# RWKV chunk chain with keys and queries side by side in the left operand, group norm by token, inversion transposes from fp16 parts

## The chip, the cores and the metric

One core of one Trainium2 chip runs the whole kernel. Five engines work side by side, each with its own list of instructions in a fixed order: TensorE (PE in the profile; its weight loads are PEld), VectorE (DVE), ScalarE (ACT), GpSimd (POOL) and SyncE (SP, which issues most of the DMAs here). They wait for each other by semaphores. The metric is the device time of one execution in microseconds; lower is better.

## What is computed

The reference is one decoder block on 512 tokens of width 2048. Two branches read the same normalised input: an RWKV-7 time mixing with 16 heads of 64 channels, and a sliding-window attention. Their gated sum is added to the input, and a gated convolutional feed-forward network follows. The change lies in the RWKV branch. Cut to that:

```python
def step(state, inp):
    r_t, k_t, v_t, w_t, ka_t, kb_t = inp          # ka = -kk, kb = kk * a
    sa = jnp.einsum('bhvk,bhk->bhv', state, ka_t)
    state = (state * w_t[:, :, None, :] + sa[..., None] * kb_t[:, :, None, :]
             + v_t[..., None] * k_t[:, :, None, :])
    y = jnp.einsum('bhvk,bhk->bhv', state, r_t)
    return state, y
...
mu = jnp.mean(y, axis=-1, keepdims=True)
var = jnp.mean(jnp.square(y - mu), axis=-1, keepdims=True)
y = ((y - mu) * lax.rsqrt(var + GN_EPS)).reshape(B, S, RW_DIM)
y = y * gn_w + gn_b
bonus = jnp.sum(rh * kh * r_k, axis=-1, keepdims=True) * vh
out = (y + bonus.reshape(B, S, RW_DIM)) * g
```

The recurrence runs over tokens; `y` is then normalised over the 64 channels of each head and token (the group norm).

## The kernel before, in words

The kernel takes two heads at a time: eight pairs, each on 128 partitions (64 per head). The 512 tokens are cut into eight chunks of 64. `early(p)` makes a pair's inputs: it projects key, receptance and value (`ztile`, three projections of 48 matmul rows each: L256 to L258), normalises the key by head, makes decays, and multiplies the bonus. The key norm is computed by matmuls with two selecting columns (`head_stats`, L330), an inverse square root on VectorE (`rsqrt_small`), a transpose (L333), and a round trip through DRAM that spreads the 8 x 128 values over partitions (`head_rows`, L337 and L341).

`late(p)` is the recurrence. It has these steps:

- `BKK` holds the two key-like vectors of both heads by channel, scaled by inverse decay; `BAR` holds the two query-like ones (`kk` and `r`), scaled by decay, with zeros where the other head's channels are. One matmul per chunk (L643) gives all products of keys and queries. Masks make `AB` (strictly lower, L646) and `MM` (with the diagonal, L647) from it.
- A triangular 64 x 64 matrix per head and chunk is inverted by doubling: levels of block size 2 to 32 (L687/L688 in fp16 with a high and a low part, `mm3`). The result is written to `BX` in fp32. After each level but the last, the whole of `BX` is transposed in fp32 (L734), and `split` makes the fp16 high part on ScalarE (L210) and the low part on VectorE (L211), which reads the high part.
- The chain over chunks. For each chunk and head: G = `AB`ᵀ`SV` (L741), where `SV` holds the state in 64 partitions and the values in the other 64; U = `BX`ᵀG (L745); the state's increment = `KK`ᵀ`UV` (L752), where `UV` holds U in 64 partitions and the values in the other 64; then the next state (L754) on VectorE. G, the increment and later y of the two heads go to the two halves of the PSUM partitions, so each of these matmuls has a 128 x 64 left operand.
- The output y = `UV`ᵀ`MM` + `SV`ᵀ`BAR` (L762, L764), also per head and chunk, comes out with channels on partitions.

`final(p)` does the group norm: a centring matmul with a 128 x 128 matrix on the high and low parts of y (L772, L773), squares, `head_stats` and `head_rows` with their DRAM round trip, then scale, shift, bonus and the output gate (`lora`), and a DMA to DRAM issued by POOL (L788).

The loop runs late(p), early(p+1), final(p) and then three gate projections. A scheduler then orders each engine's list: projections of early(p+1) and the gates stand between the small matmuls of late(p). PSUM buffers are three `bulk` tiles, three `acc` tiles and two `chn` tiles. POOL also issues the DMAs that add up pairs of weights for later stages (L232), each behind a load that SP issues (L231).

## Time and profile before

| | |
|---|---|
| median of three runs | 2905.28 us (2903.66 to 2905.93) |
| the profiled execution | 2901.93 us, its span 2900.2 us |
| granted TensorE clock, mean | 0.998 |
| RWKV stage with its pairs | about 300 to 1175 us of the span |
| L734, the inversion's fp32 transposes | 256 rows, 275 ns mean |
| L741, L752, L762, L764 together | 960 rows of 128 x 64 left operands |

How to read it: a row of the profile names the source line, the engine, the operation, the tile it writes and those it reads. An fp32 matmul stands as two rows, a transpose and an fp16 or fp32r matmul as one. Matmuls are pipelined: the duration of a row is longer than the distance to the start of the next. In the timeline, the number in front is the start in microseconds, the next is the time from there to the end of the group, and xN is how many like rows are merged. In a line of the view by windows stand the length of the window, and then for each engine the busy time and the number of instructions in it.

### The profile page before, as it was taken

Reading aid. Unit: us, or ns where it says so; the run is one execution under the profiler, and the core shown is the slowest. Engines: PE = TensorE matmul, PEld = TensorE weight load, DVE = VectorE, ACT = ScalarE, POOL = GpSimd, SP = SyncE. Lnnn points to the kernel's source line nnn. Section 1 sums busy time; section 2 is a strip of 40 time slices with the busy share of each in tenths; the row PEclk is TensorE's granted clock in tenths of the full one; section 3 lists DMA queues with packets and bytes.
Section 4 is the critical chain, followed back from the end, with each engine's and each line's share of the span. In section 5 each row is a group of like instructions: output and inputs, shape, how many; then the busy total and the mean of one; then the engine's idle time right before and its main releaser. Section 6 shows DMA issues by size and latency. Waiting matters only on the chain.

```text
span 2900.2 us, 46951 instructions
## 1 busy us (share of the span) xinstructions
PE 2854.5 (98%) x18014; PEld 2436.3 (84%) x18014; DVE 1969.8 (68%) x3383; ACT 1333.8 (46%) x2251; POOL 219.1 (8%) x286
## 2 busy tenths in 40 slices
PE   7999999999999999999999899999999999999999
PEld 5777777777777777888888899999999999888887
DVE  5577666766767766454668778777787877665555
ACT  4345435435435434322356454555545555544444
POOL 0001000000000000111000001010110100000000
PEclk9999999999999999999999999999999999999999
DMA  7865656656656655888887888898888888877775
GB/s 227 216 157 154 180 147 168 160 145 153 169 143 150 173 141 148 258 253 239 281 263 207 232 222 224 233 244 232 222 228 235 243 226 234 310 242 242 257 256 189
DMA packets 225137, 609.29 MB, mean 210 GB/s; under 512 B 24768, under 2 KB 44944, under 8 KB 223888
## 3 DMA queue, kind: packets, MB, share of 16 engines
q1 hardware_dynamic: 157504, 434.84, 46.5%
q0 software_dynamic: 36064, 132.14, 24.1%
q10 hardware_dynamic: 31344, 39.31, 4.0%
q8 instruction: 141, 2.31, 0.3%
q14 instruction: 84, 0.69, 0.1%
HBM read 556.54 MB, written 174.43 MB: 252 GB/s over the span
## 4 chain that ended last, share of the span: by engine, by line
PE 93%; DVE 2%; ACT 2%; DMA 1%; issue 1%; ACTq 0%; POOL 0%; SPq 0%; DVEq 0%; POOLq 0%
PE X L1091 17%; PE X L958 11%; PE acc L256 11%; PE acc L258 11%; PE acc L257 11%; PE Y L958 9%; PE Y L1091 8%; PE Z L1091 4%; PE bulk L734 1%; PE bulk L687 1%; PE bulk L643 1%; PE psG L741 1%; PE psS L752 1%; PE mi L460 1%; PE bulk L551 1%
## 5 line engine op out<-in xcount | busy, mean ns | idle before, releaser
L256 PE MATMUL acc<-xhi,whi 128*128 128x512 f32 x1152 | 467.9, 406 | 1.9 <-DVE xlo L303 1.9
L258 PE MATMUL acc<-xhi,wlo 128*128 128x512 f32 x1152 | 464.5, 403 | 0.0
L257 PE MATMUL acc<-xlo,whi 128*128 128x512 f32 x1152 | 463.2, 402 | 0.0
L241 ACT ACTIVATE whi<-raw 128x512 fp32r<-128x512 f32 x352 | 221.1, 630 | 490.0 <-PE acc L257 400.0
L951 DVE TENSOR_TENSOR wlo<-raw,whi 128x1024 fp32r<-128x1024 f32 x210 | 256.9, 1224 | 206.2 <-ACT whi L950 204.4
L242 DVE TENSOR_TENSOR wlo<-raw,whi 128x512 fp32r<-128x512 f32 x352 | 240.7, 689 | 205.3 <-ACT whi L241 193.4
L950 ACT ACTIVATE whi<-raw 128x1024 fp32r<-128x1024 f32 x210 | 222.7, 1061 | 287.9 <-PE X L958 146.2
L1091 PE MATMUL X<-b,whi 128*128 128x256 f32 x1472 | 270.6, 284 | 2.3 <-DVE u L1111 0.9
L1091 PE MATMUL X<-t,whi 128*128 128x256 f32 x1408 | 259.0, 284 | 8.8 <-DVE u L1111 8.3
L1074 DVE TENSOR_TENSOR wlo<-raw,whi 128x1024 fp32r<-128x1024 f32 x176 | 214.9, 1222 | 77.8 <-ACT whi L1073 77.7
L1091 PE MATMUL Y<-t,whi 128*128 128x256 f32 x1408 | 257.2, 283 | 0.0
L258 PEld LDWEIGHTS acc<-xhi,wlo 128*128 128x128 f32 x1152 | 216.6, 188 | 44.7 <-issue 3.2
L256 PEld LDWEIGHTS acc<-xhi,whi 128*128 128x128 f32 x1152 | 216.6, 188 | 44.6 <-DVE xlo L303 2.1
L257 PEld LDWEIGHTS acc<-xlo,whi 128*128 128x128 f32 x1152 | 216.8, 188 | 41.5 <-issue 3.0
L1073 ACT ACTIVATE whi<-a 128x1024 fp32r<-128x1024 f32 x132 | 139.3, 1055 | 214.3 <-DVE a L1067 212.6
L1091 PEld LDWEIGHTS X<-b,whi 128*128 128x128 f32 x1472 | 230.7, 193 | 3.1 <-issue 2.4
L1091 PEld LDWEIGHTS X<-t,whi 128*128 128x128 f32 x1408 | 221.0, 193 | 9.4 <-DVE u L1111 5.8
L1091 PEld LDWEIGHTS Y<-t,whi 128*128 128x128 f32 x1408 | 219.6, 192 | 0.0
L1091 PE MATMUL X<-b,wlo 128*128 128x256 f32 x736 | 209.1, 284 | 2.3 <-DVE wlo L1074 2.3
L1074 DVE TENSOR_TENSOR wlo<-a,whi 128x1024 fp32r<-128x1024 f32 x132 | 161.6, 1225 | 67.4 <-ACT whi L1073 66.7
L1091 PE MATMUL X<-t,wlo 128*128 128x256 f32 x704 | 200.0, 284 | 0.1
L1091 PE MATMUL Y<-t,wlo 128*128 128x256 f32 x704 | 199.2, 283 | 0.0
(345 smaller groups left out, 5875.9 us busy)
## 6 DMA issues: line engine op xcount, KB each, us to landing
raw<-in_w_up_dram SPq DMA_DIRECT2D x180, 512.0 KB
raw<-in_w_z_dram SPq DMA_DIRECT2D x288, 256.0 KB
s_dn<-in_w_dn_dram POOLq DMA_DIRECT2D x88, 512.0 KB, 6.5
raw<-in_w_up_dram POOLq DMA_DIRECT2D x88, 512.0 KB, 8.5
raw<-s_dn SPq DMA_DIRECT2D x88, 512.0 KB
raw<-in_w_dn_dram SPq DMA_DIRECT2D x66, 512.0 KB
a<-in_w_up_dram SPq DMA_DIRECT2D x48, 512.0 KB
s_dn<-in_w_dn_dram SPq DMA_DIRECT2D x44, 512.0 KB
```

The source lines that it names most:

```text
L241: act.activation(hi, raw, AF.Copy)
L242: dve.tensor_tensor(lo, raw, hi.bitcast(F32), op=ALU.subtract)
L256: pe.matmul(acc, whi[:, j], xhi[:, k], start=first, stop=False)
L257: pe.matmul(acc, whi[:, j], xlo[:, k], start=False, stop=False)
L258: pe.matmul(acc, wlo[:, j], xhi[:, k], start=False, stop=last)
L460: pe.matmul(ps, vhl[v][:, n - 1 + kb, g].rearrange("p e c -> p (e c)"), phl[p][:, kb].rearrange("p h c -> p (h c)"), start=kb == kbs[0] an ...
L950: act.activation(whi, wr, AF.Copy)
L951: dve.tensor_tensor(wlo, wr, whi.bitcast(F32), op=ALU.subtract)
L958: pe.matmul(dst, l[:, q, ts], r[:, es], start=fst and j == 0, stop=lst and j == 2, skip_group_check=True)
L1073: pin(act.activation(hi, t, AF.Copy))
L1074: pin(dve.tensor_tensor(lo, t, hi.bitcast(F32), op=ALU.subtract))
L1091: pin(pe.matmul(ps, l[:, k], r[:, k], start=start and k + i == 0, stop=last and i == 2, skip_group_check=True))
```

## The change

It does five things.

1. `BAR` is laid out so that one 128-column left operand holds, for a head, the masked key products in the rows of the other head's half and the scaled queries: `BAR[:, n, h, h]` takes `kk` in its own half and, after the L643-like matmul (now L623), the copy of `AB` in the other half; `BAR[:, n, h, 1 - h]` takes `r`. `W2` holds in the same manner the masked `MM` part and the transposed keys. So G (L729) and S (L738) are matmuls with 128 columns on the left, one per head, written next to each other in PSUM's columns. The rows of G that belong to `r`, and the rows of S that belong to `MM`, are the two terms of y. The separate output matmuls go. U (L732) has 128 columns on the right, both heads, of which half is used. y now has tokens on partitions and is added up on VectorE, twice four chunks (L748).
2. Group norm works by token: sums over 64 columns on VectorE (L756, L761) in place of centring matmuls, statistics matmuls and the DRAM round trip. y is transposed back in `final` (L770), and four ScalarE copies put it in place.
3. The inversion transposes the fp16 parts themselves (L717, into an fp16 PSUM tile), eight per level, and four copies, two on ScalarE and two on VectorE, put them into `BT`.
4. The values are transposed once from `vz` (four transposes, L659) in place of eight from `BV`; `BKK` is scaled in place instead of into `BKE`.
5. Parts of `BAR` are zeroed anew for each pair by POOL (L752), as they are now overwritten. The chain's PSUM is one buffer for G and U, and one that holds four chunks of S.

Its core:

```diff
-            BX = bdtile("BX")
-            AB, KK, SV, UV = (bd.tile([P, NCH, 2, C], F32, name=n) for n in ("AB", "KK", "SV", "UV"))
-            MM = bd.tile([P, NCH, 2, C], F32, name="MM")
+            BX, BKK = (bd.tile([P, NCH, P], F32, name=n) for n in ("BX", "BKK"))
+            W2 = bd.tile([P, NCH, 4, C], F32, name="W2")
+            GY = bd.tile([P, NCH, 2, C], F32, name="GY")
...
-                    dve.scalar_tensor_tensor(BAR[hs, :, h, 0], kk3[hs], -1.0, Eex[hs], op0=ALU.mult, op1=ALU.mult)
-                    dve.tensor_tensor(BAR[hs, :, h, 1], rz3[hs], Ein[hs], op=ALU.mult)
-                    act.activation(BV[hs, :, ol:oh], vz3[hs], AF.Copy)
+                    dve.scalar_tensor_tensor(BAR[hs, :, h, h], kk3[hs], -1.0, Eex[hs], op0=ALU.mult, op1=ALU.mult)
+                    dve.tensor_tensor(BAR[hs, :, h, 1 - h], rz3[hs], Ein[hs], op=ALU.mult)
...
-                        for g in range(2):
-                            ns = slice(g * HN, (g + 1) * HN)
-                            ps = bulk().rearrange("p (n c) -> p n c", c=P)
-                            for j in range(HN):
-                                pe.transpose(ps[:, j], BX[:, g * HN + j], ident)
-                            split(BT[:, 0, ns], BT[:, 1, ns], ps)
+                        ps = blk.tile([P, 2, NCH // 2, P], F16, name="bulk", tag="bulk")
+                        for e in (1, 0):
+                            for q in range(NCH // 2):
+                                pin(pe.transpose(ps[:, e, q], X[:, e, 2 * q : 2 * q + 2].rearrange("p n c -> p (n c)"), id16))
+                        dst = BT.rearrange("p e (q w) c -> p e q w c", w=2)
+                        for w, (rl, rh) in enumerate(HV):
+                            for h, (lo, hi) in enumerate(HV):
+                                (dve.tensor_copy if h else act.copy)(dst[lo:hi, :, :, w, lo:hi], ps[rl:rh, :, :, lo:hi])
...
                 for n in range(NCH):
-                    ps = chn.tile([P, C], F32, name="psG", tag="chn")
-                    for h, (lo, hi) in enumerate(HV):
-                        pe.matmul(ps[lo:hi], AB[:, n, h], SV[:, n, h], start=True, stop=True)
-                    G = wk.tile([P, C], F32, name="G", tag="G", bufs=2)
-                    dve.tensor_copy(G, ps)
-                    ps = chn.tile([P, C], F32, name="psU", tag="chn")
-                    pe.matmul(ps, BX[:, n], G, start=True, stop=True)
+                    ps = chn.tile([P, 2, C], F32, name="psG", tag="chn")
+                    for h in (1, 0):
+                        pin(pe.matmul(ps[:, h], BAR[:, n, h].rearrange("p a c -> p (a c)"), SV[:, n, h], start=True, stop=True))
+                    dve.tensor_copy(GY[:, n], ps)
+                    ps = chn.tile([P, 2, C], F32, name="psU", tag="chn")
+                    pe.matmul(ps.rearrange("p h c -> p (h c)"), BX[:, n], GY[:, n].rearrange("p h c -> p (h c)"), start=True, stop=True)
...
-                    for h, (lo, hi) in enumerate(HV):
-                        pe.matmul(ps[lo:hi], KK[:, n, h], UV[:, n, h], start=True, stop=True)
+                    for h in (1, 0):
+                        pin(pe.matmul(s2[:, n % HN, h], W2[:, n, 2 * h : 2 * h + 2].rearrange("p a c -> p (a c)"), UV[:, n, h],
+                                      start=True, stop=True))
...
-                        pe.matmul(dst, UV[:, n, h], MM[:, n, h], start=True, stop=n == 0)
-                        if n:
-                            pe.matmul(dst, SV[:, n, h], BAR[:, n, h, 1], start=False, stop=True)
...
+                            dve.tensor_tensor(y3[ol:oh, ns], GY[ol:oh, ns, h], s2[ol:oh, :, h], op=ALU.add)
+                if p + 1 < NP:
+                    for h in range(2):
+                        ol, oh = HV[1 - h]
+                        pool.memset(BAR[ol:oh, :, h, h], 0.0)
...
+                dve.reduce_sum(st[:, 0], y3, axis=AX.X)
+                dve.tensor_scalar(st[:, 0], st[:, 0], -1.0 / HD, None, op0=ALU.mult)
+                dve.tensor_tensor(y3, y3, st[:, 0].unsqueeze(2).to_broadcast([P, NCH, C]), op=ALU.add)
+                act.activation(sq, y, AF.Square)
+                dve.reduce_sum(st[:, 1], r3(sq), axis=AX.X)
+                rs = rsqrt_small(wk, st[:, 1], 1.0 / HD, GN_EPS)
+                dve.tensor_tensor(y3, y3, rs.unsqueeze(2).to_broadcast([P, NCH, C]), op=ALU.mult)
...
-                pe.matmul(ps, cenr, yhl[:, 0], start=True, stop=False)
-                pe.matmul(ps, cenr, yhl[:, 1], start=False, stop=True)
-                head_stats(ps, sq)
-                rb = head_rows(wk, bulk(), rs, "gn")
-                dve.tensor_tensor(yc, yc, rb, op=ALU.mult)
+                for t in range(NT):
+                    pe.transpose(ps[:, t], y[:, t * P : (t + 1) * P], ident)
```

## The prediction

> **What bounds the kernel now.** I read the page first: span, busy shares, and the shares of the chain of waits that ended last.

> ```profile
> span 2900.2 us, 46951 instructions
> PE 2854.5 (98%) x18014; PEld 2436.3 (84%) x18014; DVE 1969.8 (68%) x3383; ACT 1333.8 (46%) x2251; POOL 219.1 (8%) x286
> PE 93%; DVE 2%; ACT 2%; DMA 1%; issue 1%; ACTq 0%; POOL 0%; SPq 0%; DVEq 0%; POOLq 0%
> ```

> TensorE is hardly ever without work, so the kernel is as long as TensorE's own list of instructions. The change touches the RWKV stage, in which eight head pairs follow each other. Next I read the view of busy time by windows for one steady pair: once for everything, once for the projection rows (`acc`) alone.

> ```profile
> core 0: us, PE busy (x) PEld busy (x) DVE busy (x) ACT busy (x) POOL busy (x), PEclk, DMA share, GB/s
> 535.30:642.00 106.70, 106.56 (x701) 80.87 (x700) 72.32 (x175) 46.44 (x103) 7.08 (x9) 1.00 0.63 156
> ...
> 535.30:642.00 106.70, 78.97 (x289) 51.35 (x288) 2.24 (x3) 3.77 (x6) 1.00 0.63 156
> ```

> A pair takes 106.7 us; VectorE and ScalarE have a third and more than half of it free. Busy time can't be shared out among groups here, because neighbouring matmuls overlap in the records (a row of 0.39 us is followed by the next after 0.23). So I price everything from start to start, in the timeline of TensorE. Undisturbed projections first, and a block of eight small rows between two of them:

> ```profile
> 636.76 0.39 PE L256 MATMUL acc<-xhi,whi 128*128 128x512 f32 x1
> 636.99 0.95 PE L330 MATMUL bulk<-cst,gn 128*128 128x2 f32 x8
> 637.80 0.48 PE L257 MATMUL acc<-xlo,whi 128*128 128x512 f32 x1
> 638.12 0.39 PE L258 MATMUL acc<-xhi,wlo 128*128 128x512 f32 x1
> ...
> 641.52 0.39 PE L258 MATMUL acc<-xhi,wlo 128*128 128x512 f32 x1
> ```

> From 638.12 to 641.52 lie 15 projections: 0.227 each, so a pair's 288 take 65.3 us, and 41.4 us go to small matmuls. A block is priced from the projection ahead of it to the second one behind it, less 2 x 0.227, since its tail delays that one. For L330: 638.12 - 636.76 - 0.454 = 0.91, that is 0.113 for each full-array fp32 row (an fp32 matmul is two rows). Now one chunk of the recurrence:

> ```profile
> 615.86 0.39 PE L257 MATMUL acc<-xlo,whi 128*128 128x512 f32 x1
> 616.18 0.33 PE L752 MATMUL psS<-UV,KK 128*64 128x64 f32 x2
> 616.34 0.28 PE L762 MATMUL bulk<-MM,UV 128*64 128x64 f32 x2
> 616.46 0.28 PE L764 MATMUL bulk<-BAR,SV 128*64 128x64 f32 x2
> 616.67 0.50 PE L258 MATMUL acc<-xhi,wlo 128*128 128x512 f32 x1
> 617.01 0.39 PE L256 MATMUL acc<-xhi,whi 128*128 128x512 f32 x1
> 617.24 0.40 PE L257 MATMUL acc<-xlo,whi 128*128 128x512 f32 x1
> 617.56 0.33 PE L741 MATMUL psG<-SV,AB 128*64 128x64 f32 x2
> 617.82 0.50 PE L258 MATMUL acc<-xhi,wlo 128*128 128x512 f32 x1
> 618.25 0.33 PE L741 MATMUL psG<-SV,AB 128*64 128x64 f32 x2
> 618.51 0.51 PE L256 MATMUL acc<-xhi,whi 128*128 128x512 f32 x1
> 618.85 0.40 PE L257 MATMUL acc<-xlo,whi 128*128 128x512 f32 x1
> 619.09 0.39 PE L258 MATMUL acc<-xhi,wlo 128*128 128x512 f32 x1
> 619.32 0.33 PE L745 MATMUL psU<-G,BX 128*128 128x64 f32 x2
> 619.46 0.47 PE L256 MATMUL acc<-xhi,whi 128*128 128x512 f32 x1
> 619.77 0.40 PE L257 MATMUL acc<-xlo,whi 128*128 128x512 f32 x1
> ```

> The full-width block (L745, 128*128) costs 619.77 - 619.09 - 0.454 = 0.23. The 64-wide ones (128*64) cost far more: L741, four rows, 618.85 - 617.24 - 3 x 0.227 = 0.93; each L752/762/764 block 617.01 - 615.86 - 0.454 = 0.70, and there are two per chunk. Going from full width to 64 costs some 0.1 us (0.32 instead of 0.227 from 617.24 to 617.56), and coming back about as much again (618.25 to 618.51 is 0.26, although two 64-wide rows side by side take 0.12, 616.34 to 616.46).

> **The chain.** Each chunk now needs two G matmuls, one U and two S, all with 128 columns on the left, and no matmuls for the output at all, because rows of the same G and S results are the output. G: 4 x 0.113 = 0.45; U, now 128 columns on the right: two rows, 0.23 to 0.25; S: 0.45. That is 1.13 against 0.93 + 0.23 + 1.40 = 2.56. Not every chunk is so scattered: some blocks lie side by side or within the next pair's early steps, which saves switches. So I take the whole chain by its window, projections alone:

> ```profile
> 597.08:633.29 36.21, 23.14 (x67) 11.15 (x68) 0.75 (x1) 1.27 (x2) 1.00 0.51 122
> ```

> 36.21 - 67 x 0.227 leaves 21.0; the early steps of the next pair in it (25 rows at 0.113, and four of 512 columns at four times the 0.11 of 128 columns) are 4.6. The chain costs 16.4 plus 0.4 for the first chunk's G, which stands earlier. After: 80 rows (32 G, 16 U, 32 S, one S more than before) x 0.113 = 9.0. Saved: 7.8 us a pair.

> [...]

> **The inversion's transposes.** Per level eight fp32 transposes (L734) become eight fp16 ones, and the recomputed low part (ACT, then DVE waiting for it) becomes four plain copies that run on both engines at once.

> ```profile
> 575.12 1.05 PE L734 MATMUL bulk<-ident,BX 128*128 128x128 f32 x8
> 576.01 0.19 PE L687 MATMUL bulk<-XIW,AI 128*128 128x64 f16 x1
> 576.04 0.18 PE L688 MATMUL bulk<-XIW,AI 128*128 128x32 f16 x1
> ```

> Now 0.89 for eight, 0.111 each. An fp16 row with 128 columns isn't in the trace. Bounds: 0.03 (an fp16 row of 64 columns) and 0.111 (no gain). I take 0.057, a quarter of the 0.227 that a one-pass row of 512 columns takes. Saved per level 8 x 0.054 = 0.43, four levels 1.7 us a pair; bounds 2.6 and nothing. [...]

> **Group norm.** The centring matmuls (L772, L773: two rows shaped as a projection, 0.45), the statistics (L330, 0.91) and one transpose (L333, 0.11) go; four transposes of y come (0.44) and four of v go (0.44). Net 1.5 us. Its DMA round trip through DRAM goes too. Statistics are now made on VectorE, in free time: two reductions, some adds and a wider G copy, about 4 us more a pair against 34 free.

> **Everything else that moves** (masks, ones copied to other tiles, two POOL memsets a pair, one PSUM bank for G and U each instead of a shared pair) is off TensorE and counted at nothing; its cover is those 34 us of VectorE and 60 of ScalarE. If it fails, it shows as waits.

> Sum: 7.8 + 1.7 + 1.5 = 11.0 a pair, 88 us for eight.

> **New waits.** I read the order in which the changed kernel is built. Between G, U and S stand three to five projections as before, but two places are tighter. First, between pairs. VectorE now has the norm of pair p and the key norm of pair p+1 to do together behind the chain, and the key norm still goes through DRAM:

> ```profile
> 642.44 0.28 DVE L335 COPY rsT<-bulk 8x128 f32<-8x128 f32 x1 [0.45 <-PE bulk L333]
> 642.75 0.29 SPq L337 DMA_DIRECT2D rsd<-rsT  x1
> 646.57 1.13 SPq L341 DMA_DIRECT2D rsb<-rsd  x2
> 650.06 0.69 DVE L782 TENSOR_TENSOR yc<-yc,rsb 128x512 f32<-128x512 f32 x1 [3.61 <-DMA rsb<-rsd]
> ```

> From copy to use 7.6 us, then five VectorE steps of 0.69 until the bonus matmul can start: 11.1. TensorE has between them 33 projections, 16 rows of 0.113 and two of 512 columns, 10.2 us; and ahead of the copy I give the longer VectorE list some 0.5. I put 1.5 us on each of seven handovers. Queued behind that wait are the bonus matmul, y's transposes and all projections. Second, S now begins with the half that VectorE copies, which comes after ScalarE's:

> ```profile
> 619.93 0.23 DVE L747 COPY UV<-psU 64x64 f32<-64x64 f32 x1 [0.16 <-ACT UV L746]
> ```

> It ends 0.84 after the U block's start at 619.32; three projections and U's own rows give about 0.9. I put 0.5 us a pair on this and on the inversion's copies. Together 7 x 1.5 + 8 x 0.5 = 15. Bounds: nothing, and 5 us a pair (VectorE's list and the DMA both late).

> So 88 - 15 = 73. The profiled execution took 1.7 us more than its span, 2901.9; less 73 that is 2829. It lies 3.4 us under the median of the runs shown, 2905.3, so the median to expect is 2832.

> **Rivals.**
> - *Handovers eat half.* If the key norm's trip is late or VectorE's list longer, each pair waits about 5 us: 40 lost, 2905 - 88 + 40 = 2857. For: the trip alone is as long as the cover. Against: the list is mostly small steps that interleave.
> - *fp16 transposes cost what fp32 ones do:* 1.7 x 8 = 14 less, 2846.
> - *The 0.1 us around a 64-wide block is a wait, not the width.* Then it stays, the chain gains nothing, and 2905 - 26 + 15 = 2894. For: those blocks do wait for VectorE. Against: L745 waits likewise and pays nothing. [...]
> - *Slower: POOL's zeroing of BAR.* It needs the chain's end and must be done before the next pair's key matmuls, 66 projections and their neighbours later, about 21 us. It stands in POOL's queue behind the weight sums, whose issues wait for loads:

> ```profile
> L232 POOL DMA_DIRECT2D s_dn<-in_w_dn_dram x88 | 72.5, 824 | 1029.0 <-DMA s_dn<-in_w_dn_dram 545.0 <-DMA s_dn<-s_dn 439.5 <-DMA h_dn<-tq 33.5
> ```

> 1029 / 88 = 11.7 us each. One or two ahead of the zeroing are covered, three make it 35 - 21 = 14 late, 98 us over seven handovers, more than the 73: 2905 - 73 + 98 = 2930. It decides from 10.5 us late. Against: loads stand well ahead in the order, and much of that idle time is an empty queue.

> **Numbers.** Forecast 0.57; handovers 0.22; transposes 0.09; width no matter 0.06; POOL 0.05; the rest, 0.01, no change. The main case alone spans 2809 (no waits, cheapest transposes: 88 + 8 = 96 saved) to 2848. Below 2808 and above 2874 lies some 0.15: that is my range. Faster by over 0.2% (5.8 us, about what a measurement of this kernel can tell from no change) 0.93, within 0.02, slower 0.05.

> **What would show it.** In the profile after: pairs every 96 to 98 us; isolated G and S blocks at 0.45 and U at 0.23 by the same start-to-start price; no start of 0.32 ahead of them; eight fp16 transposes in about 0.46; TensorE idle near L591 and L623 of the changed kernel under 2 us a pair. I am wrong if G and S blocks still cost 0.7 or more, if TensorE waits 5 us at the handover (for rsb, or for POOL's memset), or if VectorE's busy share in a pair nears 90%.

## The result and the profile after

The changed kernel takes 2891.14 us (median of five runs, 2884.44 to 2892.76) against 2904.68 us for the kernel before on the same chip: ratio 0.9948, interval 0.9934 to 0.9963. That is 13.5 us less, where 73 were forecast.

The first fence is the page after: TensorE's line, then the chain of waits by engine and by line.

```profile
span 2889.4 us, 45975 instructions
PE 2812.9 (97%) x17478; PEld 2417.0 (84%) x17478; DVE 1971.8 (68%) x3423; ACT 1338.4 (46%) x2258; POOL 226.0 (8%) x299
PE 87%; DVE 7%; ACT 2%; DMA 2%; issue 1%; ACTq 0%; SPq 0%; DVEq 0%; POOLq 0%
```

TensorE has 536 rows fewer and 42 us less busy time, but the span is only 11 us shorter: VectorE's share of the chain went from 2% to 7%. The windows of four pairs, in the same columns as before, say where:

```profile
548.70:657.90 109.20, 104.56 (x645) 80.47 (x646) 73.11 (x182) 47.86 (x106) 9.07 (x12) 0.97 0.66 162
657.90:765.90 108.00, 102.46 (x635) 79.26 (x634) 73.85 (x183) 47.49 (x104) 8.39 (x11) 0.95 0.63 151
765.90:870.60 104.70, 99.88 (x634) 77.63 (x633) 71.11 (x179) 47.38 (x104) 8.41 (x11) 0.98 0.61 153
870.60:978.70 108.10, 102.17 (x633) 79.21 (x634) 72.90 (x181) 47.48 (x104) 8.11 (x11) 0.95 0.63 155
```

A pair was 106.70 us with 701 rows, 106.56 busy and the clock at 1.00. It is now 105 to 109 with some 635 rows (645 in the first window, which has 12 more projections), 4 to 6 us of it idle, and the granted clock is 0.95 to 0.98. So the list became shorter, and the time was given back twice: in waits, and in a slower clock. The view of TensorE's waits between 540 and 1170 us (six handovers) names the waits; the columns are the sum, how many, the longest. Before, this view had one wait of 0.2 us.

```profile
PE bulk L591 <- DVE lw L589: 12.5, 6, 2.8
PE acc L257 <- DVE wlo L241: 7.8, 5, 2.2
PE bulk L672 <- DVE AI L210: 3.5, 4, 0.9
PE bulk L671 <- ACT AI L209: 2.9, 4, 0.7
PE bulk L671 <- DVE XIW L210: 1.2, 5, 0.3
```

There are two places in each pair: the bonus matmul (L591) at the handover, and the start of the inversion (L671/L672, and the projections behind them, whose low weights VectorE makes late). First the handover, timeline of the chain's last matmul, of VectorE's key norm, and of TensorE:

```profile
632.02 0.66 PE L738 MATMUL psS<-UV,W 128*128 128x64 f32 x4
640.87 0.27 DVE L332 COPY rsT<-bulk 8x128 f32<-8x128 f32 x1
649.85 0.69 DVE L552 TENSOR_TENSOR kk<-kk,rsb 128x512 f32<-128x512 f32 x1 [1.79 <-DMA rsb<-rsd]
652.26 0.74 DVE L589 SCALAR_TENSOR_TENSOR lw<-rz,par,k 128x512 f32<-128x512 f32 x1
...
650.74 0.39 PE L257 MATMUL acc<-xhi,wlo 128*128 128x512 f32 x1
653.15 1.94 PE L591 MATMUL bulk<-lw,cst 128*128 128x512 f32 x2 [2.01 <-DVE lw L589]
```

The key norm's trip through DRAM takes from 640.87 to 649.85 and starts 8.9 us behind the chain's last matmul. In the kernel before the same trip lies inside the chain, and VectorE doesn't wait for it:

```profile
606.92 0.28 DVE L335 COPY rsT<-bulk 8x128 f32<-8x128 f32 x1 [0.32 <-PE bulk L333]
615.66 0.69 DVE L569 TENSOR_TENSOR kk<-kk,rsb 128x512 f32<-128x512 f32 x1
...
632.75 0.28 PE L764 MATMUL bulk<-BAR,SV 128*64 128x64 f32 x2
```

It began 25.8 us ahead of the chain's last matmul there. So the scheduler moved the next pair's key norm in the list, from inside the chain to behind it, beside the new group norm; why it did isn't shown. The waits ahead of L591 at the six handovers are 2.8, 2.0, 2.0, 1.2, 2.5 and 2.0 us. Then the start of the inversion:

```profile
670.55 0.40 PE L256 MATMUL acc<-xlo,whi 128*128 128x512 f32 x1
671.68 0.20 PE L671 MATMUL bulk<-XIW,AI 128*128 128x64 f16 x1 [0.73 <-ACT AI L209]
672.75 0.19 PE L672 MATMUL bulk<-XIW,AI 128*128 128x32 f16 x1 [0.87 <-DVE AI L210]
...
674.56 0.80 PE L257 MATMUL acc<-xhi,wlo 128*128 128x512 f32 x1 [1.45 <-DVE wlo L241]
675.15 0.63 PE L255 MATMUL acc<-xhi,whi 128*128 128x512 f32 x1
675.58 0.63 PE L256 MATMUL acc<-xlo,whi 128*128 128x512 f32 x1
```

After the wait the projections follow each other every 0.43 us, not 0.227. The windows around both places, 3.41 us each, with the granted clock (third number from the end), show it:

```profile
649.89:653.30 3.41, 1.40 (x7) 0.89 (x6) 3.41 (x6) 1.21 (x2) 0.19 (x1) 0.99 0.47 171
653.30:656.71 3.41, 3.41 (x8) 1.76 (x9) 2.97 (x5) 0.72 (x2) 0.62 (x1) 0.50 0.65 95
656.71:660.13 3.42, 3.42 (x15) 2.41 (x14) 2.57 (x5) 0.79 (x3) 0.00 (x0) 1.00 0.51 131
670.36:673.78 3.42, 1.15 (x11) 0.50 (x9) 3.11 (x7) 3.34 (x9) 0.00 (x0) 0.99 0.00 0
673.78:677.19 3.41, 2.63 (x6) 2.15 (x7) 3.24 (x8) 1.76 (x5) 0.00 (x0) 0.50 0.35 94
677.19:680.60 3.41, 3.41 (x23) 2.50 (x23) 1.36 (x3) 1.01 (x2) 0.00 (x0) 0.50 0.74 213
```

TensorE is busy for 1.40 of 3.41 us, and the next 3.41 us run at half the clock. An estimate from these lengths, half of each 3.41 us at half clock: the wait of 2.01 us costs up to 1.7 us more behind it, and the waits ahead of 673.78 twice that, as two steps at half clock follow.

The account over the seven distances from one pair's first key matmul to the next pair's, from the records of each profile: idle is the sum of the gaps between TensorE's records; half clock is the length of the stretches at 0.50, of which half counts as lost (an estimate from the 0.43 us a projection there against 0.227). Projections are counted too, because the scheduler may draw some forward from behind the last pair; those beyond the pairs' own 7 x 288 = 2016 count 0.227 us each. The list is what remains. (Gaps that the modelled ends of rows hide stay in the list, and idle time inside a half-clock stretch is counted in both.)

| profile | seven distances | idle | at half clock | projections | list, a pair |
|---|---|---|---|---|---|
| before | 748.6 | 4.4 | 0 | 2016 | 106.3 |
| after | 749.8 | 33.6 | 41.0 | 2064 | 97.8 |

The list is 8.5 us a pair shorter; 4.2 of idle, 2.9 of clock and 1.6 of projections drawn forward eat it whole. The 48 projections, 10.9 us, all run in the first three distances, and that work is missing behind the last pair's key matmuls: from there to the end it is 1817.2 us before and 1802.5 after, so 3.8 of these 14.7 us are a gain. Without the projections drawn forward the seven distances gain 9.7 us.

### The profile page after: what moved, and what is told of

Read it like the earlier page. It is cut to its first block, busy times and chain, and to the rows that moved or that the text cites. A ratio compares the mean times of both kernels' runs of the same rounds, so it can differ in the third digit from the quotient of the medians.

```text
span 2889.4 us, 45975 instructions
## 1 busy us (share of the span) xinstructions
PE 2812.9 (97%) x17478; PEld 2417.0 (84%) x17478; DVE 1971.8 (68%) x3423; ACT 1338.4 (46%) x2258; POOL 226.0 (8%) x299
## 3 DMA queue, kind: packets, MB, share of 16 engines
q8 instruction: 137, 2.24, 0.3%
## 4 chain that ended last, share of the span: by engine, by line
PE 87%; DVE 7%; ACT 2%; DMA 2%; issue 1%; ACTq 0%; SPq 0%; DVEq 0%; POOLq 0%
PE X L1085 16%; PE X L952 11%; PE acc L255 10%; PE acc L257 10%; PE acc L256 9%; PE Y L952 9%; PE Y L1085 8%; PE Z L1085 4%; PE psS L738 1%; DMA rsb<-rsd 1%; PE psG L729 1%; PE bulk L623 1%; PE bulk L534 1%; PE bulk L671 1%; DVE wlo L241 1%
## 5 line engine op out<-in xcount | busy, mean ns | idle before, releaser
L257 PE MATMUL acc<-xhi,wlo 128*128 128x512 f32 x1152 | 466.5, 405 | 7.8 <-DVE wlo L241 7.8
L256 PE MATMUL acc<-xlo,whi 128*128 128x512 f32 x1152 | 468.5, 407 | 0.0
L257 PEld LDWEIGHTS acc<-xhi,wlo 128*128 128x128 f32 x1152 | 220.0, 191 | 50.9 <-DVE wlo L241 8.7
L256 PEld LDWEIGHTS acc<-xlo,whi 128*128 128x128 f32 x1152 | 219.7, 191 | 38.9 <-issue 1.6
```

The source lines that it names most:

```text
L256: pe.matmul(acc, whi[:, j], xlo[:, k], start=False, stop=False)
L257: pe.matmul(acc, wlo[:, j], xhi[:, k], start=False, stop=last)
```

## The experiments

The theory after this reading: the shorter list is real, two waits per pair and the half clock behind them give it back. The rivals: the clock falls for another reason (the short fp16 transposes); VectorE's longer list and not the trip sets the handover; the shorter list is worth little in itself. Ratios are against the kernel before on the same chip. Seven distances compare only with the projections beside them: each one beyond 2016 is 0.227 us of later work done early.

| run | us | ratio, interval | seven distances | idle | at half clock | projections |
|---|---|---|---|---|---|---|
| `e1_no_trip` | 2865.4 | 0.9861, 0.9844 to 0.9879 | 729.8 | 20.7 | 3.4 | 2087 |
| `e2_filler` | 2888.8 | 0.9944, 0.9928 to 0.9960 | 751.1 | 21.6 | 10.2 | 2094 |
| `e7_dve_later` | 2910.9 | 1.0019, 1.0009 to 1.0028 | 767.7 | 51.6 | 34.1 | 2064 |
| `e10_all` | 2863.4 | 0.9853, 0.9836 to 0.9869 | 719.9 | 20.7 | 3.4 | 2051 |
| `e5_before_fp16` | 2900.1 | 0.9982, 0.9973 to 0.9992 | 745.4 | 5.2 | 3.4 | 2016 |
| `e6_keys_early` | 2850.5 | 0.9808, 0.9793 to 0.9822 | 697.8 | 14.0 | 0 | 2016 |
| `e9_both_keys` | 2842.7 | 0.9782, 0.9768 to 0.9797 | 694.7 | 8.2 | 0 | 2016 |
| `e14_start_light` | 2844.7 | 0.9790, 0.9775 to 0.9804 | 694.6 | 8.0 | 0 | 2016 |
| `e17_fp32_back` | 2856.9 | 0.9827, 0.9811 to 0.9844 | 705.4 | 7.0 | 0 | 2016 |
| `e4_four_gates` | 2902.1 | 0.9982, 0.9973 to 0.9992 | 784.9 | 18.5 | 3.4 | 2352 |

**The trip taken away.**

```diff
-                rb = head_rows(wk, bulk(), rs, "lg")
+                rx = wtile("lg")
+                act.copy(rx.rearrange("p (t h c) -> p t h c", t=NT, h=2),
+                         rs.rearrange("p (h t) -> p t h", h=2).unsqueeze(3).to_broadcast([P, NT, 2, HD]))
+                rb = bulk()
+                for t in range(NT):
+                    pe.transpose(rb[:, t * P : (t + 1) * P], rx[:, t * P : (t + 1) * P], ident)
```

> The changed kernel, but the inverse norms of the keys are spread over the partitions by four TensorE transposes of a ScalarE copy instead of by the round trip through DRAM; the result is the same. Theory (two waits per pair, one at the handover and one at the start of the inversion, and after each a window at half the granted clock): the wait of 2.0 us ahead of the bonus matmul goes and with it the half-clock window behind it, some 1.7 us, less 0.33 for three more transposes; seven handovers give about 23 us, 2868 (2860 to 2880), and one half-clock window per pair instead of two. Rival A (the half clock comes from something else, the short fp16 transposes or the shorter list): the windows stay, 7 x 1.7 = 12 us, about 2879. Rival B (VectorE's longer list, not the trip, sets the handover): 2888 to 2893, with TensorE still waiting for the bonus product.

2865.4, near the 2868 of the theory. TensorE's waits in this run, same stretch of time:

```profile
PE bulk L676 <- ACT AI L209: 4.8, 3, 1.8
PE bulk L645 <- DVE BX L639: 2.9, 2, 1.5
PE acc L257 <- DVE wlo L241: 2.9, 4, 1.9
PE bulk L596 <- DVE lw L594: 2.8, 6, 0.5
```

The wait ahead of the bonus matmul (L596 here) falls from 12.5 to 2.8 us over six handovers, though VectorE's list is shorter by one copy of 0.27 us only: rival B falls. Half-clock time falls from 41.0 to 3.4 us, more than expected; the waits that are left are 1.9 us at most. The fp16 transposes are all still there: rival A falls.

**Filler ahead of the bonus matmul.**

```diff
+                for i in range(3 if p else 0):
+                    pe.matmul(ps, K["bo"], kb, start=True, stop=True)
                 pe.matmul(ps, K["bo"], rk, start=True, stop=True)
```

> The changed kernel with three idle fp32 matmuls of 512 columns (0.45 us each) put ahead of the bonus matmul, into the tile that it overwrites; they wait for kb, which is ready about 1.3 us before the bonus product. 7 x 1.4 = 9.5 us more TensorE work, no wait taken away at its source. Theory (TensorE's idle time in a window is what halves the clock of the next one): at the handover TensorE idles 1.2 us or less instead of 2.0, the half-clock window there vanishes, and with more work the kernel becomes faster by 5 to 12 us, 2879 to 2886. Rival A (the clock has another cause): the windows stay, 2890 to 2900.

2888.8: it doesn't tell the theories apart. The scheduler put the filler not behind the 28 projections but behind 22, so TensorE waits for `kb` instead:

```profile
650.73 5.46 PE L592 MATMUL bulk<-kz,cst 128*128 128x512 f32 x6 [4.29 <-DVE kz L587]
```

The waits at the start of the inversion are gone (15.4 us over six pairs in the changed kernel, 1.1 with the filler). Between the two groups of the first level's matmuls (L671/L672 of the changed kernel) now stand 10 to 14 projections, where four of the changed kernel's eight pairs have three: the six left over from the handover, and more that were drawn forward (78 over the seven distances, against 48). So more projections are enough to cover that place.

**VectorE's jobs at the start of the inversion moved back.** The mask of BT, the scaling of BKK, and the transposes of BKK and the values, in program order:

```diff
-                dve.tensor_tensor(BKK, BKK, ee.unsqueeze(2).to_broadcast([P, NCH, P]), op=ALU.mult)
-                    for i in range(2):
-                        dve.tensor_tensor(BT[:, i, ns], AI[:, i, ns], mb("t1bd", HN), op=ALU.mult)
...
+                    if m == LEVELS[2]:
+                        values()
```

> The changed kernel with three jobs moved behind the first doubling level of the inversion: the scaling of BKK in place (1.2 us on VectorE), the transposes of BKK and of the values with their ScalarE copies; and the mask of BT (2.6 us on VectorE) moved behind AI's. No work is added or removed. Theory (at the start of the inversion VectorE's list is late, then the clock halves): the waits of 0.7, 0.9 and 1.5 us there shrink to 1 us in all and the half-clock window goes, 8 x (2 + 2) = 30 us, 2861 (2850 to 2875). Rival A (clock has another cause): 16 us, 2875. Rival B (the wait only moves to the second half of the level): 2885 to 2895.

2910.9, slightly slower than the kernel before and 20 us slower than the changed one: a miss for every theory stated. The waits:

```profile
PE acc L257 <- DVE wlo L241: 14.8, 5, 3.7
PE bulk L591 <- DVE lw L589: 11.8, 6, 3.0
PE bulk L649 <- DVE XIW L210: 7.7, 8, 2.1
```

The largest wait, 3.6 to 3.7 us in four of the pairs, is one place further on, ahead of the first level's second half (the products with BT), as rival B said of the place but not of the time:

```profile
679.28 0.79 PE L257 MATMUL acc<-xhi,wlo 128*128 128x512 f32 x1 [3.58 <-DVE wlo L241]
```

In VectorE's list the scaling of BKK and the mask of BT now stand shortly ahead of these low weights (673.47 to 677.90, the weights from 678.54). On TensorE one projection stands ahead of that second half in these pairs, ten in the same pairs of the changed kernel, and the transposes that stood ahead of the first half as cover are gone too. What was taken from VectorE in one place came back in the next, and some of TensorE's cover went with it; the two weren't separated.

**Both cures, and the key norm traced ahead of the chain.** `early` is cut in two; its first part, up to the normalised key, is called in `late` ahead of the loop over chunks:

```diff
+                if p + 1 < NP:
+                    ks.append(keys(p + 1))
                 y = wtile("yc")
                 y3 = r3(y)
                 for n in range(NCH):
```

> The changed kernel with both cures, and the next pair's key norm traced ahead of the chain, so that it runs between the chain's steps. Theory: no wait over 1 us and no half-clock window in the RWKV stage; the shorter list then shows, pairs every 96 to 99 us, 2825 to 2845. Rival (the shorter list is worth little, or the early steps delay the chain): 2860 or more, pairs above 103 us without half-clock windows.

2863.4, the rival's time, with pairs of 102.3 to 104.1, mostly just under the rival's 103, and one half-clock step. As the run before made clear, one of its cures does harm, so the next runs separate them; without it (`e9_both_keys`) the same kernel takes 20.7 us less.

**One part of the change alone, in the kernel before.** The two hunks of the diff that concern `id16` and L717.

> The kernel before with one part of the change alone: the inversion's eight transposes per level made from the fp16 parts, with four plain copies behind them. Theory (a shorter TensorE list comes through one to one where it brings no new wait): 0.41 us a level, four levels, eight pairs, 13 us, 2893 (2888 to 2898), no half-clock window in the RWKV stage. Rival A (the fp16 transposes themselves bring waits or the half clock): 2900 to 2910.

2900.1: the time is outside the theory's range and at the near end of rival A's, but the steady pairs speak against rival A. They fall from 106.7 to 105.6, and the view of TensorE's waits from 540 to 1150 us lists none, as before: 1.1 us a pair, less than the 1.64 expected. The first distance is 3.7 us longer than before and holds the only half-clock step of the stage; why isn't shown. So there is no new wait from the part itself in the steady pairs.

**Order alone.** The cut of `early` as above, with the trip through DRAM kept and the inversion as in the changed kernel.

> The changed kernel with one difference of order: the next pair's key projection and key norm, with its trip through DRAM, are traced ahead of the chain over chunks instead of behind it, so that they run between the chain's steps, as the kernel before had them. Theory (at the handover the change left the key norm's trip and the group norm one behind the other): the handover's wait and its half-clock window go, 7 x 3.7 = 26 us, about 2865, as without the trip. Rival (the trip now stalls VectorE inside the chain): the chain takes some 5 us longer per pair, 2885 or more.

2850.5: the instructions of the changed kernel, 40 us faster by their order. The trip stands in the chain again:

```profile
588.48 0.28 DVE L332 COPY rsT<-bulk 8x128 f32<-8x128 f32 x1 [0.36 <-PE bulk L330]
596.25 0.69 DVE L552 TENSOR_TENSOR kk<-kk,rsb 128x512 f32<-128x512 f32 x1 [0.84 <-DMA rsb<-rsd]
```

VectorE waits 0.84 us for it and the chain with it (4.7 us over five pairs, longest 1.7): the rival's effect exists and is a fifth of what it supposed. No half-clock stretch is left in the stage. This run also closes the account: the same instructions, with 2016 projections and no half clock, leave a list of 97.7 us a pair, against the 97.8 worked out above for the changed kernel.

**Order, and no trip.**

> The key norm ahead of the chain and its rows spread by transposes instead of the trip; the inversion as in the changed kernel. Theory: no wait at the handover, what is left are the waits at the start of the inversion with their clock, so between 2845 and 2860; if those waits go too, because more projections are left over for them, 2835. Rival (in the version with both cures it was the early key norm that cost): 2865 or more.

2842.7, the best of all, 2.2% under the kernel before, and under the changed kernel with no overlap of intervals. Two pairs by windows:

```profile
540.00:639.30 99.30, 98.14 (x637) 77.17 (x636) 74.03 (x180) 47.41 (x106) 8.13 (x11) 1.00 0.66 163
639.30:738.60 99.30, 98.14 (x637) 77.16 (x636) 74.16 (x180) 47.37 (x106) 8.16 (x11) 1.00 0.67 160
```

Pairs of 99.3, clock 1.00, 98.14 of it busy. The waits at the start of the inversion shrank without being touched, from 15.4 to 3.4 us over six pairs, 0.6 at most. Each pair has its own 288 projections as a stock: between the chain's end and the key matmuls the changed kernel spends 66 (33, 5 and 28 in its list), this one 37, and where four of the changed kernel's pairs have three projections between the two groups of the first level's matmuls (L671/L672), this one has eleven. The stock is only half of it: the kernel before spent 86 at the first place and had two at the second, without a wait. There VectorE had the second half of AI ready 12.6 us behind the pair's first key matmul; in the changed kernel it is 14.8, in this one 14.4. So the change makes VectorE 2.2 us later at this place, and the eleven projections cover it.

**The same with VectorE relieved at the start of the inversion,** BT's mask and BKK's scaling behind AI.

> The same, and at the start of the inversion the masks of BT and the scaling of BKK stand behind AI on VectorE, but ahead of the transposes of BKK and the values. Theory: AI is ready 2.5 us earlier, the waits there shrink to below 1 us a pair: 2835 to 2850. Rival (whatever is taken from VectorE there, the scheduler leaves fewer projections as cover, and the wait stays): within 5 us of the version without this.

2844.7 and the same pairs, inside both ranges: the wait there, 3.4 us over six pairs, becomes 3.2. The scheduler leaves six projections between the two groups instead of eleven, as the rival had it.

**The fp16 part undone in the best version.**

```diff
-                                pin(pe.transpose(ps[:, e, q], X[:, e, 2 * q : 2 * q + 2].rearrange("p n c -> p (n c)"), id16))
...
+                                pe.transpose(ps[:, j], BX[:, g * HN + j], ident)
+                            split(BT[:, 0, ns], BT[:, 1, ns], ps)
```

> The version with the key norm ahead of the chain and without the trip, with one part of the change undone: the inversion's transposes are fp32 again, from BX, with the split behind them. Theory (in a list without waits a part is worth what it takes off TensorE): pairs of 100.4 instead of 99.3 us, as the same part alone took 106.7 to 105.6 in the kernel before; 9 us, 2851 to 2853. Rival (the forecast's 0.43 a level): 14 us, 2856 to 2858. Rival B (the fp16 parts are worth nothing where other engines set the level): within 4 us of 2843.

2856.9, 14 us more, the time of the rival and of the forecast's own price. The pairs say a little less: 100.8 (705.4 over seven) against 99.3, so 1.5 us each, between the theory's 1.1 and the forecast's 1.7. That is 12 us for eight pairs; in the two profiles 2.7 us lie behind the last projection, where the edit changes nothing. The same part is worth 1.1 us a pair in the old list and 1.5 in the new one.

**More projections in each pair.**

```diff
-GATES_PER_PAIR = 3
+GATES_PER_PAIR = 4
```

> The changed kernel with four gate projections a pair instead of three, so 48 more projections of 0.227 in each pair and none left for behind the stage; no work is added. Theory (the handover lacks no projections as such; the key norm's trip stands behind the chain, and the ones there are ahead of the bonus matmul stay 28): the handover's wait of 2.0 us and its half clock stay, the waits at the start of the inversion shrink, since more projections are left for it: 2870 to 2888. Rival A (the pairs are only short of projections): both waits go, 2840 to 2860. Rival B (what the gates covered behind the stage is laid bare): 2890 or more.

2902.1, rival B for the time, the theory for the places. Handover waits stay (10.2 us over six), those at the start of the inversion shrink to 2.4. Against the theory only one half-clock step is left in the seven distances. What the gates had covered behind the last pair is laid bare:

```profile
1140.00:1174.60 34.60, 31.75 (x274) 24.67 (x272) 20.79 (x49) 18.55 (x43) 1.46 (x2) 1.00 0.57 149
1174.60:1215.60 41.00, 22.93 (x74) 17.05 (x73) 14.01 (x49) 3.66 (x12) 0.00 (x0) 0.50 0.09 26
```

With nothing but the chain's own small matmuls TensorE is busy for 22.93 of 41.00 us, at half the clock throughout.

## Why the prediction was wrong, step by step

- *TensorE's list bounds the kernel, so a shorter list shortens it.* Right, as `e9_both_keys` shows: with most of the waits gone the time falls by 63 us.
- *The chain, 7.8 us a pair.* The mechanism held, the size was off. Start to start, from the best version:

```profile
606.01 0.40 PE L257 MATMUL acc<-xhi,wlo 128*128 128x512 f32 x1
606.25 0.58 PE L738 MATMUL psG<-SV,BAR 128*128 128x64 f32 x4
606.64 0.48 PE L255 MATMUL acc<-xhi,whi 128*128 128x512 f32 x1
606.96 0.39 PE L256 MATMUL acc<-xlo,whi 128*128 128x512 f32 x1
607.18 0.39 PE L257 MATMUL acc<-xhi,wlo 128*128 128x512 f32 x1
607.41 0.38 PE L741 MATMUL psU<-GY,BX 128*128 128x128 f32 x2
607.55 0.48 PE L255 MATMUL acc<-xhi,whi 128*128 128x512 f32 x1
607.87 0.39 PE L256 MATMUL acc<-xlo,whi 128*128 128x512 f32 x1
608.10 0.40 PE L257 MATMUL acc<-xhi,wlo 128*128 128x512 f32 x1
608.36 0.66 PE L747 MATMUL psS<-UV,W 128*128 128x64 f32 x4
608.83 0.48 PE L255 MATMUL acc<-xhi,whi 128*128 128x512 f32 x1
609.15 0.39 PE L256 MATMUL acc<-xlo,whi 128*128 128x512 f32 x1
```

  G 606.96 - 606.01 - 0.454 = 0.50 (0.45 forecast), U 607.87 - 607.18 - 0.454 = 0.24 (0.23 to 0.25), S 609.15 - 608.10 - 0.454 = 0.60 (0.45); over all blocks of the changed kernel 0.49, 0.24 and 0.58. Eight chunks take 10.5, not 9.0, so the chain gives 6.3. Width did cost what was said: the rival that laid the 0.1 us around a 64-wide block to a wait falls; no run shows a chain that gains nothing, as it had it, but these 6.3. G has four rows a chunk before and after; at full width they cost 0.49, which is the rows' own 0.45 and 0.04 around them, where the 64-wide ones cost 0.93. S took 0.70 + 0.70 and takes 0.58. Why S costs more than G isn't settled; in the changed kernel's single records its first two rows start mostly 0.16 us apart, those of G 0.09.
- *fp16 transposes, 1.7.* Right: eight of them go by in 0.46 us, as forecast, and undoing them cost 1.5 us a pair. The rival falls.
- *Group norm, 1.5.* Not tried alone. By the account the list is 106.3 - 98.1 = 8.2 us a pair shorter in the best version, which has three transposes (0.33) more: 8.5, as in the changed kernel itself, against the 11.0 of the sum. The chain explains 1.5 of the difference, the fp16 part 0.2; 0.8 stays open.
- *Everything else at nothing.* Wrong at one place: VectorE has the second half of AI ready 2.2 us later than before, and the low weights behind it come late too, 15.4 us of waits over six pairs where too few projections are left to cover it.
- *New waits, 15 us: 7 x 1.5 at the handover and 8 x 0.5.* This is the step that failed. The right place was named first, the key norm behind the chain together with the group norm, and the wait there, 2.1 us, is near the 1.5 assumed. But three things were missed. A wait was priced by its idle time alone, although the windows of the profile have the clock in them: 41 us of half clock are 20 us lost. That the inversion's start would come to need cover too, and that the projections spent at the handover would be lacking there, was not considered. And that the trip had lain inside the chain before (606.92 to 615.66) was not set against its new place, which would have shown that the order, not the trip, was what changed. Idle and clock together take 54 us over seven distances, 7.7 a pair where 2.0 were allowed, and more than the 5 of the rival "handovers eat half". That rival had the place and the cause, but of the idle time only 2.1 us a pair lie at the handover; the start of the inversion and the clock are in no rival.
- *The sum.* Over the seven distances 7 x 9.0 = 63 us less were forecast and 1.2 more came. Of these 64, idle and clock beyond the 14 allowed (and beyond the 4.4 before) are 35.7, the list that is 2.5 a pair longer than forecast is 17.6, and the projections drawn forward are 10.9; these last come back behind the stage.
- *POOL's zeroing.* No wait of TensorE or of the steps that write `BAR` was for POOL; the rival that was slower falls.

By its own signs: pairs came every 105 to 109 us, not 96 to 98; U and the transposes came as said, G and S some 0.05 to 0.15 dearer; the idle time at L591 alone was 2.1 a pair. None of the three signs named for being wrong came: no block at 0.7, no wait of 5 us at the handover, VectorE busy for 67 to 68% of a pair.

## What to carry to other kernels

Where a scheduler orders the lists, a change of one part moves others: compare where the long trips of the neighbouring part begin, before and after, and if one has left its cover, trace it ahead of what it must overlap; here this order alone was worth 40 us, three times what the whole change had brought. Work that covers waits is a stock: count where it is spent, since what one place takes the next one lacks, and count it too before two profiles are compared stretch by stretch, since a scheduler may have drawn later work into one of them. And read the granted clock beside the idle time: here the wait of 2.01 us ahead of the bonus matmul was followed by 3.41 us at half clock, by estimate up to 1.7 us more.

## What the runs showed of the hardware

```
busy share   steps   the next step at half clock
0.0 to 0.4      54      54
0.4 to 0.5      27      19
0.5 to 0.6      28       3
0.6 to 0.9     206       0
0.9 to 1.0    9593       0
```

So in these profiles the next step was at half clock after all 54 steps with a busy share below 0.4, after 19 of 27 between 0.4 and 0.5, after 3 of 28 between 0.5 and 0.6, and after none above that. What decides between 0.4 and 0.6 isn't shown. The length of a wait alone doesn't tell: of the changed kernel's six handovers, the longest wait, 2.80 us up to 545.42, lies across two steps (from 540.66 and 544.07) that were busy for 1.96 and 2.06 us, and no half clock followed; that of 1.97 us up to 1082.05 lies in one step (from 1079.97) that was busy for 1.45 us, and half clock followed.
